# Moving one small transfer, the weights and the latents' blocks in the opening of a two-layer attention kernel

## The chip, the cores and the metric

The kernel is one program on one core of a Trainium2 chip. The metric is the device time of that program in microseconds; runs are compared by their medians. The engines named below are PE (matrix products, with its weight loads PEld), DVE, ACT and POOL (elementwise work, reductions and activation functions), and SP, whose queue issues most of the transfers.

## The reference

Two trunk layers work on 512 latent tokens and 256 context tokens of width 1024. Each layer normalises both streams, modulates them with a scale and a shift computed from a conditioning vector (one vector for the latents, one for the context), and projects them to 4608 columns. Three groups of heads attend on parts of that projection, a gate multiplies the result, and an output projection is added back. The part that matters here stands at the start of layer 0:

```
mod = c_silu @ ada_w + ada_b                     # shift, scale, gate, each 1024 wide
hx = rmsnorm(x, norm_w) * (1 + scale) + shift    # latents, 512 tokens
hc = rmsnorm(cx, norm_w) * (1 + scale_c) + shift_c   # context, 256 tokens
px = split_cols(hx @ w_in)
pc = split_cols(hc @ w_in)
rmsnorm(x, w) = x * rsqrt(mean(x*x) + 1e-6) * w
```

Group A also normalises its queries and keys per head with two rows of 64 weights per layer, and group C has one sink logit per head. These 272 numbers are the small input `bcast`.

## The kernel before

Activations lie with the 1024 features on partitions, as eight blocks of 128 features (index `kt`), and the tokens along the free axis: 512 columns of latents and 256 of context. All products are made in three passes of a rounded high part and a low part (`hh`, `hl` for activations, `wh`, `wl` for weights): high by high, high by low, low by high. `split` (line 244) makes the weight parts: a copy on ACT (line 247) and a subtraction (line 250, on DVE in the opening).

The opening of layer 0 (lines 381 to 461) runs like this.

- SP issues its transfers in the order of the program, one queue, with eight semaphores in turn, so that a ninth transfer waits for the first to land. In that order come `sm` (small constants), `bc` (the 272 numbers, spread over 128 partitions by an access pattern with a step of zero, line 81), the eight latent blocks `x` of 256 KB (`load_x(0)`), the first modulation weights `ada` (two halves of 512 KB), the eight context blocks of 128 KB (`load_x(1)`), and from there modulation weights of later blocks and projection weights `ws` of 256 KB.
- `norm_x` makes the sums of squares: for each block ACT squares it (line 351), and DVE adds the square onto the first one (line 355), so that seven additions follow each other. The squares have three buffers, of which one holds the sum. Then PE adds over partitions with a vector of ones (line 359), DVE and POOL make the inverse root (lines 366 and 369), PE spreads it over all partitions (line 378), and ACT copies it to `rb` (line 401).
- `ada(kt)` makes the modulation of one feature block: PE products in two halves (line 214), an ACT copy `adasb` (line 218), PE transposes (line 222), DVE sums and additions (lines 225 to 231).
- `make_h(kt, s)` makes the high and low part of one block of stream `s`: DVE scales `x` in place (line 408), ACT adds the shift and rounds to `hh` (line 409). For half of the blocks DVE makes `hl` (line 411), for the others POOL does it in two steps (lines 413 and 414): the latents of even `kt` go to DVE, those of odd `kt` to POOL. `wrap_h` repeats 64 columns of the latents.
- For each `kt`, PE then adds that block's products to eight open accumulators (line 430): `q` and `k` of head group B for latents (512 columns, in `pj`) and context (256, in `Obig`), and `v` per token tile (in `Sbig`). The contraction runs over `kt`, so no result is ready before the eighth block.
- `spread_silu` transposes the conditioning vector in four pieces (line 135), copies them on ACT (line 138) and stores them for later.

A tile scheduler places each engine's instructions by data, buffers and priorities, at build time. Each engine runs its list strictly in order. From the end of this opening on, PE has product after product, in both layers.

Of the kernel before, what the change touches and what calls it, by code (L numbers as in the profile page):

```python
# [15 lines left out]
OP = mybir.AluOpType  # L16
# [5 lines left out]
NT = 512  # L22
NCX = 256
# [34 lines left out]
BC_N = 272  # L58
# [5 lines left out]
def body(tc, xT, small, bcast, rpb, adaw, adat, wt, wf, wo, trigA, trigC, mskB, mskC, outT):  # L64
    nc = tc.nc
# [12 lines left out]
    sm = const.tile([128, SM_N], F32)  # L78
    nc.sync.dma_start(sm, small)
    bc = const.tile([128, BC_N], F32)  # L80
    nc.sync.dma_start(bc, bass.AP(tensor=bcast.tensor, offset=bcast.offset, ap=[[0, 128], [1, BC_N]]))
    ones = const.tile([128, 2], F32)
    nc.vector.memset(ones, 1.0)
    mhalf = const.tile([128, 8], F32)
# [1 line left out]
    onesw = const.tile([128, 64], F32)  # L86
    nc.vector.memset(onesw, 1.0)
    negsink = const.tile([128, 16], F32)
    nc.vector.tensor_scalar(negsink, bc[:, BC_SINK:BC_SINK + 16], -1.0, None, op0=OP.mult)

    def pj():
        return ps.tile([128, 512], F32, name="pj", bufs=CFG["pj"])
# [102 lines left out]
    def ada_load(k, pool, tag, bufs):  # L195
        sts = []
        for half in range(2):
            st = pool.tile([128, 4, 256], F32, name="ada", tag=tag, bufs=bufs)
            nc.sync.dma_start(st, adaw[k, half])
            sts.append(st)  # L200
        return sts
# [52 lines left out]
    def load_w1(dram_ap, i, shape):  # L254
        st = wpool.tile([128, 512], F32, name="ws", bufs=CFG["ws"])
        pace["sp"] = nc.sync.dma_start(st, dram_ap[:, i * 512:(i + 1) * 512]).ins.name
        return split(st, shape)
# [14 lines left out]
    def en(kind):  # L272

        turn[kind] = turn.get(kind, -1) + 1
        return nc.vector if EN[kind][turn[kind] % len(EN[kind])] == "D" else nc.gpsimd
# [14 lines left out]
    def wrap_h(kt):  # L290
        for h in (hh, hl):
            t = h[kt][2]
            nc.scalar.activation(t[:, 0:64], t[:, NT:NT + 64].bitcast(F32), AF.Copy)
# [7 lines left out]
    def off_tile(h, t):  # L301

        return h[2][:, t * 128:t * 128 + 128] if t < 4 else cols(h, t * 128, 128)
# [41 lines left out]
            with tc.high_priority(offset=CFG["hp"]):  # L345
                done(p[:, 0:512].rearrange("p (t c) -> p t c", t=2), t2)

    def add_sq(sums, x, kt, n, pool, bank=psO):

        sq = pool.tile([128, NT], F32, name="sq", bufs=3)  # L350
        nc.scalar.activation(sq[:, 0:n], x, AF.Square)
        if kt == 0:
            sums.append(sq)
            return
        en("sq").tensor_add(sums[0][:, 0:n], sums[0][:, 0:n], sq[:, 0:n])
        if kt == KT - 1:
            pss = bank()
            for t in range(n // 128):
                nc.tensor.matmul(pss[:, 2 * t:2 * t + 2], sums[0][:, t * 128:(t + 1) * 128], ones,
                                 start=(t == 0), stop=True, skip_group_check=True)  # L360
            sums.append(pss)
# [22 lines left out]
    with tc.tile_pool(name="p0", bufs=1, reuse_waits="tile") as p0:  # L384
# [3 lines left out]
        def load_x(s):  # L388
            c0, c1 = SETS[s]
            for kt in range(KT):  # L390
                x = p0.tile([128, c1 - c0], F32, name=f"x{s}", bufs=8)
                nc.sync.dma_start(x, xT[kt * 128:(kt + 1) * 128, c0:c1])
                xs[s, kt] = x

        def norm_x(s):
            n = SETS[s][1] - SETS[s][0]
            sums = []
            for kt in range(KT):
                add_sq(sums, xs[s, kt], kt, n, p0, lambda: Obig[:, s * 8:])
            r = p0.tile([128, n], F32, name=f"rb{s}")  # L400
            nc.scalar.activation(r, rstd_rows(sums[1], n, p0, Sbig[:, s * 512:s * 512 + n])[:, 0:n], AF.Copy)
            rb[s] = r
# [11 lines left out]
                nc.gpsimd.tensor_sub(hl[kt][s], x, hh[kt][s].bitcast(F32))  # L414


        load_x(0)
        sts = {0: ada_load(0, p0, "ada", CFG["a0"])}
        load_x(1)
        norm_x(0)  # L420
        norm_x(1)
        early["f", WF_BQ] = [pj(), Obig[:, 0:256]]
        early["f", WF_BK] = [pj(), Obig[:, 256:512]]
# [12 lines left out]
        for kt in range(KT):  # L436
            if kt < KT - 1:
                sts[kt + 1] = ada_load(kt + 1, p0, "ada", CFG["a0"])
            if kt % 4 == 0:
                wq = {s: load_w1(wf[0, s], kt // 4, (4, 128)) for s in (WF_BQ, WF_BK)}  # L440
            if kt % 2 == 0:
                wv = load_w1(wt[0, WT_BV, kt // 4], kt // 2 % 2, (2, 256))
            hh[kt], hl[kt] = new_h(), new_h()
            with tc.high_priority(offset=CFG["h1"]):
                ada(kt, sts.pop(kt), psT)
                for s in range(2):
                    make_h(kt, s)
                wrap_h(kt)
            for x, s in enumerate((WF_BQ, WF_BK)):
                wh, wl = wq[s]  # L450
                for g, (c0, n) in enumerate(((0, NT), (NT, NCX))):
                    for i, (a, b) in enumerate(((wh, hh), (wh, hl), (wl, hh))):
                        part(("c", 0) if g else ("l", x), early["f", s][g][:, 0:n], a[:, kt % 4, :], cols(b[kt], c0, n),
                             kt, i)
            wh, wl = wv
            for t in (1, 2, 3, 4, 5, 0):
                p = early["t", WT_BV][t // 2][:, t % 2 * 256:t % 2 * 256 + 256]
                for i, (a, b) in enumerate(((hh, wh), (hh, wl), (hl, wh))):
                    part(("v", t // 2), p, off_tile(a[kt], t), b[:, kt % 2, :], kt, i)
            if kt in (1, 2, 3, 4):  # L460
                spread_silu(kt - 1, p0)

# [1208 lines left out]
```

## Time and profile before

| | |
|---|---|
| median of 3 runs (lowest, highest) | 1202.65 us (1200.88, 1202.7) |
| span of the profiled execution | 1197.7 us |
| own time of the profiled execution | not given beside its span; the median of the runs lies 4.95 us above that span |
| PE, PEld busy | 1150.5 us (96%), 1034.8 us (86%) |
| DVE, ACT, POOL busy | 769.4 us (64%), 696.9 us (58%), 408.1 us (34%) |
| moved by transfers | 124.22 MB |

All times inside the program count from the start of the span. A row of the timeline gives start, duration, engine, line, operation, the tiles written and read, the shape and a count; rows of equal instructions that follow each other are merged, and the bracket at the end tells how long the engine had been idle and what ended that. A group row gives the busy time of a line's instructions and the mean nanoseconds of one. The chain of waits follows the work back from the last instruction, each step to what released it.

### The profile page before, as it was taken

How to read it: one execution, taken by the hardware profiler on the slowest of the kernel's cores; microseconds unless marked ns; L12 is line 12 of the kernel's file. 1: busy time of each engine (PE TensorE's matmuls, PEld its weight loads, DVE VectorE, ACT ScalarE, POOL GpSimd, SP SyncE). 2: the span in 40 equal slices, each digit the busy share in tenths (PEclk: the TensorE clock that was granted, in tenths of full speed). 3: DMA queues.
4: the chain of work that ended last, by engine and by line, in shares of the span. 5: the costliest groups of instructions: out<-in, count | busy, mean ns of one | idle time of the engine just before them, and what ended most of it. 6: DMA issues, size and time to landing. Idle time of an engine off the chain costs nothing.

```text
span 1197.7 us, 21749 instructions
## 1 busy us (share of the span) xinstructions
PE 1150.5 (96%) x8016; PEld 1034.8 (86%) x8016; DVE 769.4 (64%) x1548; ACT 696.9 (58%) x1581; POOL 408.1 (34%) x496
## 2 busy tenths in 40 slices
PE   5999999999999999999999999999999999998997
PEld 3898999998898988988778999989988888887876
DVE  5767566764656665568578895567754556567563
ACT  5446555656666676588423544555666667677552
POOL 1341110234446354385000030202274563656001
PEclk9999999999999999999999999999999999999999
DMA  9552222313312112123086662323222111232152
GB/s 321 213 142 89 78 78 67 123 66 104 111 70 92 67 44 92 34 63 119 27 293 198 205 210 74 98 84 109 91 73 67 53 46 53 63 88 72 36 161 77
DMA packets 60826, 124.22 MB, mean 104 GB/s; under 512 B 7216, under 2 KB 13488, under 8 KB 60720
## 3 DMA queue, kind: packets, MB, share of 16 engines
q1 hardware_dynamic: 54768, 111.96, 29.6%
q10 hardware_dynamic: 5952, 10.88, 2.7%
q8 instruction: 63, 1.03, 0.3%
q14 instruction: 43, 0.35, 0.1%
HBM read 109.05 MB, written 11.14 MB: 100 GB/s over the span
## 4 chain that ended last, share of the span: by engine, by line
PE 81%; DVE 5%; ACT 5%; DMA 3%; issue 3%; POOL 1%; SPq 0%; ACTq 0%; DVEq 0%; POOLq 0%
PE pj L318 18%; PE pj L341 17%; PE Sbig L1049 9%; PE Obig L1049 9%; PE T L1054 9%; PE pj L519 5%; PE T L519 3%; PE Sbig L519 3%; PE T L341 2%; PE Sbig L430 2%; DVE ptl L1044 1%; DMA x<-xT_dram 1%; PE Sbig L341 1%; ACT pth L798 1%; PE pj L430 1%
## 5 line engine op out<-in xcount | busy, mean ns | idle before, releaser
L1044 DVE TENSOR_TENSOR ptl<-T,pth 128x512 fp32r<-128x512 f32 (+2 forms) x312 | 181.1, 591 | 128.6 <-ACT pth L798 126.7
L798 ACT ACTIVATE pth<-T 128x512 fp32r<-128x512 f32 (+2 forms) x312 | 158.9, 520 | 134.8 <-PE T L1054 128.1
L341 PE MATMUL pj<-wh,hL 128*128 128x256 f32 x896 | 180.6, 287 | 0.0
L318 PE MATMUL pj<-hL,wh 128*128 128x512 f32 x544 | 175.0, 401 | 0.9 <-ACT wh L247 0.5
L1054 PE MATMUL T<-ident,P 128*128 128x128 f32 x1024 | 165.7, 273 | 4.0 <-ACT qt L902 1.7
L247 ACT ACTIVATE wh<-ws 128x512 fp32r<-128x512 f32 x192 | 119.5, 629 | 78.6 <-PE pj L318 16.3
L1049 PE MATMUL Sbig<-kt,qt 128*128 128x256 f32 (+1 forms) x864 | 156.2, 308 | 4.6 <-ACT P L1160 2.5
L250 POOL TENSOR_TENSOR wl<-ws,wh 128x512 fp32r<-128x512 f32 x76 | 98.5, 1300 | 146.4 <-ACT wh L247 146.4
L341 PEld LDWEIGHTS pj<-wh,hL 128*128 128x128 f32 x896 | 144.2, 190 | 1.0 <-issue 0.2
L1049 PE MATMUL Obig<-pth,vt 128*128 128x256 f32 (+2 forms) x432 | 134.6, 321 | 4.6 <-ACT pth L798 2.0
L1054 PEld LDWEIGHTS T<-ident,P 128*128 128x128 f32 x1024 | 123.0, 140 | 17.6 <-DVE ptl L1044 2.2
L1049 PE MATMUL Obig<-ptl,vt 128*128 128x256 f32 (+2 forms) x432 | 131.4, 318 | 5.0 <-DVE ptl L1044 4.3
L1049 PEld LDWEIGHTS Sbig<-kt,qt 128*128 128x128 f32 x864 | 123.3, 189 | 13.4 <-DVE negm L1208 4.1
L341 PE MATMUL pj<-wl,hL 128*128 128x256 f32 x448 | 128.0, 286 | 0.0
L318 PEld LDWEIGHTS pj<-hL,wh 128*128 128x128 f32 x544 | 96.2, 189 | 16.7 <-ACT wh L247 0.9
L250 DVE TENSOR_TENSOR wl<-ws,wh 128x512 fp32r<-128x512 f32 x116 | 82.7, 720 | 40.4 <-ACT wh L247 31.6
L318 PE MATMUL pj<-hL,wl 128*128 128x512 f32 x272 | 107.1, 394 | 0.5 <-DVE wl L250 0.5
L1049 PEld LDWEIGHTS Obig<-pth,vt 128*128 128x128 f32 x432 | 81.6, 189 | 15.9 <-ACT pth L798 7.1
L1049 PEld LDWEIGHTS Obig<-ptl,vt 128*128 128x128 f32 x432 | 81.5, 189 | 14.7 <-DVE ptl L1044 11.3
L1445 POOL TENSOR_TENSOR bm<-wr,bm 128x192 f32<-128x192 f32 (+1 forms) x48 | 41.3, 888 | 139.6 <-DMA bm<-mskB_dram 132.4
L341 PEld LDWEIGHTS pj<-wl,hL 128*128 128x128 f32 x448 | 85.4, 191 | 0.3
L1158 DVE TENSOR_REDUCE negm<-Sbig 128x1 f32<-128x768 f32 x64 | 61.0, 953 | 29.7 <-PE Sbig L1049 15.7
(336 smaller groups left out, 2495.6 us busy)
## 6 DMA issues: line engine op xcount, KB each, us to landing
ws<-wf_dram SPq DMA_DIRECT2D x72, 256.0 KB, 3.1
ws<-wt_dram SPq DMA_DIRECT2D x72, 256.0 KB, 3.0
ada<-adaw_dram SPq DMA_DIRECT2D x32, 512.0 KB, 5.5
ws<-wo_dram SPq DMA_DIRECT2D x57, 256.0 KB, 2.8
bm<-mskB_dram SPq DMA_DIRECT2D x16, 576.0 KB, 3.7
dw<-adat_dram SPq DMA_DIRECT2D x8, 512.0 KB, 8.2
dots<-adat_dram SPq DMA_DIRECT2D x16, 256.0 KB, 4.5
u<-u ACTq DMA_DIRECT2D x9, 384.0 KB, 2.9
```

The costliest lines, as they stand in the source:

```text
L247: nc.scalar.activation(hi, src, AF.Copy)
L250: eng.tensor_sub(lo, src, hi.bitcast(F32))
L318: paced(nc.tensor.matmul(p[:, 0:n], a[:, r, :], cols(b[kt], c0, n), start=(i == 0), stop=(i == 23)), i)
L341: paced(nc.tensor.matmul(p[:, t * 256:(t + 1) * 256], tok(a[kt], t2 + t), b[:, r, :], start=(i == 0), stop=(i == 23)), i)
L430: mm = nc.tensor.matmul(out, a, b, start=begin, stop=(kt == KT - 1 and i == 2), skip_group_check=True)
L519: mm = nc.tensor.matmul(p[:, 0:n], a[:, r, :], ucols(ua[b][ft], c0, n), start=(ft == FT_ORDER[0] and i == 0), stop=(ft == FT_ORDER[-1] and ...
L798: nc.scalar.activation(out, src, AF.Copy)
L1044: i = nc.vector.tensor_sub(lo[:, 0:n], T[:, 0:n], hi[:, 0:n].bitcast(F32))
L1049: m = nc.tensor.matmul(*args, **kw)
L1054: m = nc.tensor.transpose(*args, **kw)
L1158: nc.vector.tensor_reduce(nm, S, axis=AX.X, op=OP.max, negate=True)
L1445: nc.gpsimd.tensor_add(b, src, b)
```

## The change

- The row `bc` is no longer spread by the access pattern at the head of SP's queue. The host repeats the 272 numbers 128 times, and a plain transfer brings them in when the fifth feature block (`kt == 4`) is built; the small operation on it (`negsink`) goes with it.
- The seven additions of the latents' squares are cut by columns: DVE adds columns 0 to 383, POOL columns 384 to 511. The context's stay whole on DVE.
- `norm_x(0)` and the weights of the first block come before `load_x(1)` in the program, so the three `ws` transfers and their splitting stand ahead of the context's transfers and squares.
- `wrap_h` follows the latents directly, and for each `kt` all latent products (`q`, `k`, `v`) come before all context products.

```diff
-    nc.sync.dma_start(bc, bass.AP(tensor=bcast.tensor, offset=bcast.offset, ap=[[0, 128], [1, BC_N]]))
...
-    nc.vector.tensor_scalar(negsink, bc[:, BC_SINK:BC_SINK + 16], -1.0, None, op0=OP.mult)
...
-    def add_sq(sums, x, kt, n, pool, bank=psO):
+    def add_sq(sums, x, kt, n, pool, bank=psO, cut=0):
...
-        en("sq").tensor_add(sums[0][:, 0:n], sums[0][:, 0:n], sq[:, 0:n])
+        if cut:
+            nc.gpsimd.tensor_add(sums[0][:, cut:n], sums[0][:, cut:n], sq[:, cut:n])
+        nc.vector.tensor_add(sums[0][:, 0:cut or n], sums[0][:, 0:cut or n], sq[:, 0:cut or n])
...
-                add_sq(sums, xs[s, kt], kt, n, p0, lambda: Obig[:, s * 8:])
+                add_sq(sums, xs[s, kt], kt, n, p0, lambda: Obig[:, s * 8:], 0 if s else 384)
...
+        def load_weights(kt):
+            if kt % 4 == 0:
+                wq.update({s: load_w1(wf[0, s], kt // 4, (4, 128)) for s in (WF_BQ, WF_BK)})
+            if kt % 2 == 0:
+                wq["v"] = load_w1(wt[0, WT_BV, kt // 4], kt // 2 % 2, (2, 256))
+
+        wq = {}
         load_x(0)
         sts = {0: ada_load(0, p0, "ada", CFG["a0"])}
+        norm_x(0)
+        load_weights(0)
         load_x(1)
-        norm_x(0)
         norm_x(1)
...
+            if kt == 4:
+                nc.sync.dma_start(bc, bcast)
+                nc.vector.tensor_scalar(negsink, bc[:, BC_SINK:BC_SINK + 16], -1.0, None, op0=OP.mult)
...
                 for s in range(2):
                     make_h(kt, s)
-                wrap_h(kt)
-            for x, s in enumerate((WF_BQ, WF_BK)):
-                wh, wl = wq[s]
-                for g, (c0, n) in enumerate(((0, NT), (NT, NCX))):
+                    if s == 0:
+                        wrap_h(kt)
+            for g, (c0, n) in enumerate(((0, NT), (NT, NCX))):
+                for x, s in enumerate((WF_BQ, WF_BK)):
+                    wh, wl = wq[s]
...
-            for t in (1, 2, 3, 4, 5, 0):
-                p = early["t", WT_BV][t // 2][:, t % 2 * 256:t % 2 * 256 + 256]
+                wh, wl = wq["v"]
+                for t in ((4, 5) if g else (1, 2, 3, 0)):
+                    p = early["t", WT_BV][t // 2][:, t % 2 * 256:t % 2 * 256 + 256]
...
-    bcast = np.concatenate([q_norm_a.ravel(), k_norm_a.ravel(), sink_c.ravel()])
+    bcast = np.tile(np.concatenate([q_norm_a.ravel(), k_norm_a.ravel(), sink_c.ravel()]), (128, 1))
```

The scheduler turns this into other lists. At the head of SP's queue, before (128x512 are latent blocks, 128x256 context blocks):

```order
L79 DMA sm<-small_dram 128x88
L81 DMA bc<-bcast_dram 128x272
L392 DMA x_113<-xT_dram 128x512
...
L392 DMA x_127<-xT_dram 128x512
L199 DMA ada<-adaw_dram 128x1024 x2
L392 DMA x_133<-xT_dram 128x256
...
L392 DMA x_147<-xT_dram 128x256
L199 DMA ada<-adaw_dram 128x1024 x2
L256 DMA ws<-wf_dram 128x512 x2
L256 DMA ws<-wt_dram 128x512
```

And in the change:

```order
L79 DMA sm<-small_dram 128x88
L392 DMA x_111<-xT_dram 128x512
...
L392 DMA x_125<-xT_dram 128x512
L197 DMA ada<-adaw_dram 128x1024 x2
L254 DMA ws<-wf_dram 128x512 x2
L254 DMA ws<-wt_dram 128x512
L392 DMA x_192<-xT_dram 128x256
...
L392 DMA x_206<-xT_dram 128x256
L197 DMA ada<-adaw_dram 128x1024 x6
```

The row `bc` is gone from second place (it now stands as the 36th transfer), and the three `ws` went from behind the context's blocks and the second block's modulation weights to a place ahead of both.

On ACT, from the last square of a latent block to the first rounded block `hL`, before (`rb_176` is the latents' inverse root, `adasb` the copy for the modulation, `spr` a piece of `spread_silu`):

```order
L351 ACTIVATE sq<-x_127 128x512
L351 ACTIVATE sq<-x_133 128x256
...
L351 ACTIVATE sq<-x_139 128x256
L218 ACTIVATE adasb<-T 128x256
L351 ACTIVATE sq<-x_141 128x256
...
L351 ACTIVATE sq<-x_147 128x256
L401 ACTIVATE rb_176<-Sbig 128x512
L138 ACTIVATE spr<-T 128x512
L409 ACTIVATE hL<-x_113,mod_0_98 128x512
L247 ACTIVATE wh<-ws 128x512
```

In the change:

```order
L349 ACTIVATE sq<-x_125 128x512
L245 ACTIVATE wh<-ws 128x512 x2
L216 ACTIVATE adasb<-T 128x256
L245 ACTIVATE wh<-ws 128x512
L349 ACTIVATE sq<-x_192 128x256
L349 ACTIVATE sq<-x_194 128x256
L401 ACTIVATE rb_165<-Sbig 128x512
L349 ACTIVATE sq<-x_196 128x256
L349 ACTIVATE sq<-x_198 128x256
L136 ACTIVATE spr<-T 128x512
L349 ACTIVATE sq<-x_200 128x256
L409 ACTIVATE hL<-x_111,mod_0_96 128x512
```

The three weight copies moved ahead of `rb`; of the context's eight squares, two stand ahead of `rb`, three between `rb` and `hL`, and three behind.

On PE, from the start to the second feature block's modulation, before (`L214` are modulation products, `L359` the sums over partitions, `L430` the blocks' products):

```order
L214 MATMUL T<-ada,silu_c 2x256 x4
L359 MATMUL Obig<-ones,sq 128x2 x4
L214 MATMUL T<-ada,silu_c 2x256 x4
L222 MATMUL T<-ident,adasb 128x128 x2
L378 MATMUL Sbig<-ident,rstd 128x128 x4
L135 MATMUL T<-ident,silu_c 128x128 x4
L214 MATMUL T<-ada,silu_c 2x256 x4
L359 MATMUL Obig<-ones,sq 128x2 x2
L214 MATMUL T<-ada,silu_c 2x256 x4
L430 MATMUL pj<-hL,wh 128x512 x2
L222 MATMUL T<-ident,adasb 128x128 x2
```

In the change:

```order
L359 MATMUL Obig<-ones,sq 128x2 x4
L212 MATMUL T<-ada,silu_c 2x256 x8
L378 MATMUL Sbig<-ident,rstd 128x128 x4
L220 MATMUL T<-ident,adasb 128x128 x2
L133 MATMUL T<-ident,silu_c 128x128 x4
L438 MATMUL pj<-hL,wh 128x512 x2
...
L212 MATMUL T<-ada,silu_c 2x256 x4
L359 MATMUL Obig<-ones,sq 128x2 x2
L212 MATMUL T<-ada,silu_c 2x256 x8
L220 MATMUL T<-ident,adasb 128x128 x2
```

Before the first `pj` product the change has one block's modulation and the latents' sums; the second block's modulation (8), the context's sums (2) and the third block's modulation now stand between the first `pj` product and the second block's transposes (the last row), where before those transposes followed the first two products at once. Behind the opening the lists of all engines are the same but for a few neighbours that change places.

More of the change, by code (lines that the diff above doesn't have):

```diff
@@ L438, in body @@
                 sts[kt + 1] = ada_load(kt + 1, p0, "ada", CFG["a0"])
[L439 to L442, printed above, removed]
+            if kt:
+                load_weights(kt)
+            if kt == 4:
+                nc.sync.dma_start(bc, bcast)
+                nc.vector.tensor_scalar(negsink, bc[:, BC_SINK:BC_SINK + 16], -1.0, None, op0=OP.mult)
             hh[kt], hl[kt] = new_h(), new_h()
@@ L454, in body @@
                              kt, i)
-            wh, wl = wv
-            for t in (1, 2, 3, 4, 5, 0):
-                p = early["t", WT_BV][t // 2][:, t % 2 * 256:t % 2 * 256 + 256]
-                for i, (a, b) in enumerate(((hh, wh), (hh, wl), (hl, wh))):
-                    part(("v", t // 2), p, off_tile(a[kt], t), b[:, kt % 2, :], kt, i)
+                wh, wl = wq["v"]
+                for t in ((4, 5) if g else (1, 2, 3, 0)):
+                    p = early["t", WT_BV][t // 2][:, t % 2 * 256:t % 2 * 256 + 256]
+                    for i, (a, b) in enumerate(((hh, wh), (hh, wl), (hl, wh))):
+                        part(("v", t // 2), p, off_tile(a[kt], t), b[:, kt % 2, :], kt, i)
             if kt in (1, 2, 3, 4):
```

## The prediction

> **What bounds the kernel now.** I read the page first, for the engine that fills the span.
>
> ```profile
> PE 1150.5 (96%) x8016; PEld 1034.8 (86%) x8016; DVE 769.4 (64%) x1548; ACT 696.9 (58%) x1581; POOL 408.1 (34%) x496
> PE 81%; DVE 5%; ACT 5%; DMA 3%; issue 3%; POOL 1%; SPq 0%; ACTq 0%; DVEq 0%; POOLq 0%
> ```
>
> PE is busy 96% of the span and holds 81% of the chain that ends last. The change adds and removes no product, so it can gain only where PE waits. The chain in order of time shows where, in the opening:
>
> ```profile
> 2.58 5.51 DMA x<-xT_dram
> ...
> 8.11 6.29 DMA x<-xT_dram
> ...
> 15.36 6.04 DMA ws<-wf_dram
> ...
> 21.42 0.64 ACT wh L247
> ...
> 22.10 0.74 PE pj L430 x2
> ...
> 30.18 0.69 DVE mod L231
> ...
> 31.55 0.73 ACT hL L409
> 32.29 0.04 issue
> 32.33 0.74 PE pj L430 x2
> ...
> 33.89 0.83 PE Sbig L430 x7
> ```
>
> The first real product starts at 22.10, released by a weight copy that waited for its transfer. A second stall ends at 32.33. By stages:
>
> ```profile
> 22.10:32.33 10.23, 9.66 (x70) 5.70 (x71) 7.44 (x19) 5.38 (x14) 5.06 (x5) 1.00 1.03 407
> 32.33:69.08 36.75, 36.75 (x302) 32.28 (x303) 23.01 (x51) 18.09 (x45) 15.59 (x14) 1.00 0.54 181
> ```
>
> From 32.33 to the end of the opening PE is busy 36.75 of 36.75 us. So what the change is worth is how much earlier PE reaches the state that it has at 32.33: two latent products of the third block next, nothing missing any more.
>
> **The change, part by part.**
>
> *The row bc.* What the head of the queue costs stands in the transfers' list and in two stretches of 2.20 to 5.60 and 5.60 to 13.60 (last number: GB/s):
>
> ```profile
> bc<-bcast_dram SPq DMA_DIRECT2D x1, 136.0 KB, 4.8
> sm<-small_dram SPq DMA_DIRECT2D x1, 44.0 KB, 1.8
> 2.20:5.60 3.40, 0.00 (x0) 0.00 (x0) 0.65 (x6) 0.22 (x1) 0.00 (x0) 1.00 0.82 135
> 5.60:13.60 8.00, 0.73 (x8) 0.14 (x8) 5.02 (x8) 5.04 (x8) 0.00 (x0) 1.00 1.05 394
> 6.73 2.75 ACT L351 ACTIVATE sq<-x 128x512 f32<-128x512 f32 x4 [4.00 <-DMA x<-xT_dram]
> 8.12 5.47 DVE L355 TENSOR_TENSOR sq<-sq 128x512 f32<-128x512 f32 x7 [1.99 <-ACT sq L351]
> 9.65 0.63 ACT L351 ACTIVATE sq<-x 128x512 f32<-128x512 f32 x1 [0.17 <-DVE sq L355]
> ```
>
> While `bc` is under way the queue moves 135 GB/s, afterwards 394. ACT gets its first latent block at 6.73. Without `bc` ahead, the first block is issued when `bc` was, at about 1.17 (chain: 1.64 less one issue of 0.47), and lands after 1.8 (as `sm` did) and 256 KB at 394 GB/s (0.66): at 3.5 to 3.6. I take 3.5; bounds 3.2 to 4.2. That is 3.2 us earlier. The later load of `bc` I cost at nothing. 10.25 MB stand ahead of it in the queue, so at 394 GB/s it lands near 29.6; DVE comes to `negsink` behind the fourth block's scaling, near 32, and by its place in the order PE then has some 59 products of 0.12 (chain: 0.83 by seven) in hand. If that cover failed, DVE's next low part, queued behind `negsink`, would wait, and PE for it, at most for the 4.8 that `bc` takes now.
>
> *The additions cut by columns.* Now each takes 0.78 (5.47 by seven). For the new pair the trace has these rows:
>
> ```profile
> L355 DVE TENSOR_TENSOR sq<-sq 128x512 f32<-128x512 f32 x14 | 9.6, 689 | 4.1 <-ACT sq L351 3.4
> L355 DVE TENSOR_TENSOR sq<-sq 128x256 f32<-128x256 f32 x14 | 5.9, 421 | 2.5 <-ACT sq L351 2.3
> L1340 POOL TENSOR_TENSOR tR<-onesw,rec 128x128 f32<-128x128 f32 x30 | 11.1, 404 | 0.3 <-DVE rec L1327 0.3
> 550.99 1.28 POOL L492 TENSOR_TENSOR hL<-uf,hL 128x512 fp32r<-128x512 f32 x1 [0.90 <-ACT hL L491]
> 551.75 0.80 DVE L492 TENSOR_TENSOR hC<-uf,hC 128x256 fp32r<-128x256 f32 x1
> ```
>
> DVE alone would need 0.555 for 384 columns (middle of 0.689 and 0.421), POOL 0.40 for 128. But the last two rows show them in each other's way: POOL works until 552.27, and the DVE subtraction, which alone takes 0.42, starts inside that time and ends at 552.55, 0.28 after POOL. So DVE's reading waits for POOL's end, and only 0.14 of it lies beside. A pair then takes 0.40 + 0.555 − 0.14 = 0.82. The square after next needs the buffer that both release: 0.06 to start (the row at 9.65, behind the addition that ends at 8.12 + 0.78 + 0.69), 0.63 on ACT, 0.13 until DVE starts (8.12 after two squares from 6.73), and the pair's 0.82 make 1.64 for two pairs, 0.82 for each. I take that, so the cut gains nothing. The second block lands 0.66 after the first, at 4.17; the first addition starts at 4.17 + 0.63 + 0.13 = 4.93, and the last pair ends at 4.93 + 6 × 0.82 + 0.82 = 10.7, before 13.59: 2.9 us earlier. Bounds: without that wait 0.69 each, ending at 9.6; with the 0.1 that lies between two additions now (0.78 less 0.69) behind each pair, 0.92, ending at 11.3. Nothing else is queued on POOL then. The Trainium skill (SBUF — State Buffer, "Who interferes with whom") says that a DVE instruction with two SBUF inputs and a POOL instruction that reads SBUF exclude each other for the whole of the instruction; by that the pair would take 0.96, each step 0.89 by the same buffer sum, the last pair would end at 11.2, and the forecast would be 0.5 us higher. The row's 0.14 beside the other speaks for the smaller figure.
>
> *From the sums to the first product.* The rows:
>
> ```profile
> 12.87 1.03 PE L214 MATMUL T<-ada,silu_c 128*2 128x256 f32 x8 [12.87 <-DVE sq L355]
> 13.83 1.87 PE L359 MATMUL Obig<-ones,sq 128*128 128x2 f32 x8
> 15.98 1.03 POOL L369 TENSOR_TENSOR rstd<-rstd,mhalf 128x4 f32<-128x4 f32 x1 [14.70 <-DVE rstd L366]
> 18.89 0.58 ACT L401 ACTIVATE rb<-Sbig 128x512 f32<-128x512 f32 x1
> 20.41 0.72 ACT L409 ACTIVATE hL<-x,mod 128x512 fp32r<-128x512 f32 x1
> ```
>
> PE's sums (1.87) run to 12.5, and now both halves of the first modulation follow them (0.96 each from start to start of the next, 12.87 to 13.83) to 14.4; the root (1.03) is ready by 13.9, beside them. ACT, in order, waits for that modulation, copies it (0.4) to 14.9, then makes the third weight copy (0.6) and two context squares (0.4 each) before `rb` from 16.3 to 16.9. DVE, which has the modulation's sums and two context additions ahead, scales the block from 17.7 to 18.3; ACT meanwhile has two squares, `spr` and another square, and `hL` lasts from 18.6 to 19.35. First product at 19.4, 2.7 earlier than now. What releases PE today, the weights, has 3.25 MB up to its first block in the new queue: at 394 GB/s it lands near 11, and is copied before `rb`. That wait is gone, and `hL` is late next. The context's blocks land up to 2 us later for that (0.75 MB), from 13.3 on; ACT wants the first near 15.5.
>
> *From there to the steady state.* What PE waits for in this stretch is the second block's low part, made on POOL:
>
> ```profile
> 22.68 0.38 PE L222 MATMUL T<-ident,adasb 128*128 128x128 f32 x2
> 24.84 0.74 DVE L408 SCALAR_TENSOR_TENSOR x<-x,mod,rb 128x512 f32<-128x512 f32 x1
> 25.62 0.72 ACT L409 ACTIVATE hL<-x,mod 128x512 fp32r<-128x512 f32 x1 [0.51 <-DVE x L408]
> 26.45 2.48 POOL L413 TENSOR_SCALAR x<-x,mod 128x512 f32<-128x512 f32 x2 [3.68 <-ACT hL L409]
> 28.89 1.27 POOL L414 TENSOR_TENSOR hL<-x,hL 128x512 fp32r<-128x512 f32 x1
> ```
>
> It is ready at 30.16. In the change more stands on PE between the first product and the transposes (L222): two products and a half modulation to 20.3, when the first block's low part is there; four products (0.9), the other half (0.5), the context's sums (0.5), the third block's modulation (1.0). So the transposes start near 23.3 instead of 22.68. From there to DVE's scaling it takes 2.2 today (22.68 to 24.84), with two weight subtractions between, each as long as an addition of 512 columns (0.7), which in the change are done by then; 2.2 less 1.4, and 0.2 for waits, is 1.0: 24.3. ACT has three copies ahead of `hL` (25.2 to 25.9); POOL takes the same 3.7: ready at 29.8, only 0.4 earlier. Four products (0.9 with their start) follow to 30.9. In the old order the same products are followed by a wait until 32.33 for the third block. Here the third block's modulation is made with the second's, so its high part is ready near 28.2 and its low part near 30.6, and PE goes on. 32.33 − 30.9 = 1.4 us.
>
> The other half, context products behind latent ones, moves no count: the same 30 products for each block. Behind the opening the lists are the same, so 1.4 reaches the end: span 1197.7 − 1.4 = 1196.3, and with the 4.95 that the runs' median lies above this span, 1201.3. Own range: gain 0.5 to 2.3, 1200.4 to 1202.2.
>
> A measurement of this kernel tells about 0.2%, 2.4 us, from no change.
>
> **The rivals.**
>
> 1. The start is carried in full: POOL's low part isn't what PE waits for (its transposes come earlier than I placed them), and PE is dense from 19.4. Then the gain is 2.7 at the first product, and up to 3.5 with the 0.57 that PE isn't busy between 22.10 and 32.33: 1199.2 to 1200.0. For it: the transfers of the second and third block's modulation come 2 to 5 us earlier, since weights and `bc` are out of their way. Against: the order of PE. Chance 0.26.
> 2. DVE and POOL add side by side: 1.0 more, gain 2.4, 1200.3, half of it over the bound. Against: the pair at 551. Chance 0.12.
> 3. The clock, slower than before. These rows are at the layer's end and in the opening (the number before the last two is the granted clock):
>
> ```profile
> 621.76:625.17 3.41, 0.79 (x3) 0.35 (x3) 3.37 (x7) 1.46 (x3) 0.00 (x0) 1.00 1.02 375
> 625.20:628.50 3.30, 3.30 (x8) 2.63 (x9) 3.30 (x6) 1.26 (x2) 0.00 (x0) 0.50 1.01 367
> 18.57 1.06 PE L135 MATMUL T<-ident,silu_c 128*128 128x128 f32 x4
> 23.88 0.60 PE L135 MATMUL T<-ident,silu_c 128*128 128x128 f32 x4
> ```
>
> After 3.4 us with PE busy 0.79, the granted clock was 0.50 for 3.3 us. The same four transposes took 1.06 at 18.57 and 0.60 at 23.88: PE sped up between, just before its first product. In the change PE has nothing to do from about 17.5 to 19.4 and less fill work before. If it then runs at half speed for one stretch of 3.4 us, 1.7 less 0.5 of slack are lost, gain 0.2 (1202.4); for two, 3.4 less 0.5, a loss of 1.5 (1204.1); from 8.7 us at half speed it passes the bound. The Trainium skill (TensorE: Matmul & The Clock Gate, part 1) says that the clock is raised after one busy window of about 3.4 us and lowered after an idle one, with windows that run freely; by that rule one window is the usual price. The trace's 3.3 us at 0.50 agree. Chance 0.12, of which 0.05 over the bound.
> 4. The change doesn't do what it says: the first transfers crawl whatever they are, and the blocks come only 0.35 earlier (136 KB at 394 GB/s). Then nothing is left, 1202.6. Against: `sm` landed in 1.8. Chance 0.06.
>
> **How the numbers follow.** The forecast has 0.44: 1201.3. Faster by over 0.2% (under 1200.25): 0.26 of rival 1, 0.06 of rival 2, 0.02 of the forecast's edge, 0.34. Slower by over 0.2%: 0.05. The rest, 0.61, is the same. Range: down to rival 1 with its first block at the early bound (1199.0), up past one slow stretch of the clock, half-way to two (1203.3).
>
> **What would show it.** Right: first `x` lands near 3.5; the pairs of additions every 0.8, DVE's or POOL's stretched over 0.55 or 0.40; first product near 19.4; a wait of PE for POOL's `hL` (L414) near 29 to 30; dense from there. Wrong: additions ending before 10 (rival 2), no such wait and a dense PE from 20 (rival 1), products of 512 columns that take twice as long after 19 (rival 3), a first block after 5 (rival 4), or a difference behind 70 us that the opening does not have.

## The result and the profile after

| | before | changed |
|---|---|---|
| median of 6 runs each, side by side | 1200.81 us | 1205.12 us |
| ratio of the runs, 95% interval | | 1.0038 (1.0024 to 1.0051) |
| span of the profiled execution | 1197.7 us | 1203.7 us |

The change makes the kernel slower by 0.38%, some 4.5 us (4.3 between the medians); the forecast was 1.4 us faster. Two single runs on record, one of the kernel before (1894.1 us) and one of an experiment below (row and cut additions, 2284.5 us), lie far off all others and enter no ratio. The first lines of the changed kernel's page: PE does the same 8016 products, and DMA and POOL have taken some of its share of the chain.

```profile
PE 1153.2 (96%) x8016; PEld 1036.6 (86%) x8016; DVE 770.8 (64%) x1548; ACT 697.2 (58%) x1581; POOL 415.4 (35%) x503
PE 79%; DVE 6%; ACT 5%; DMA 4%; issue 3%; POOL 3%; SPq 0%; ACTq 0%; DVEq 0%; POOLq 0%
```

I read the end of the opening at the first product of the projection behind it. The row of the chain before, and that of the changed kernel:

```profile
86.12 5.47 PE pj L318 x24
```
```profile
90.61 5.47 PE pj L316 x24
```

It comes 4.49 later: in these two executions the opening loses as much as the medians do. (The two spans differ by 6.0: this execution was at half clock for 6.8 us near 629 and for 3.4 us near 1014, the one before for 3.4 us near 625; such stretches come and go between executions.) The chain of the changed kernel in order of time:

```profile
2.58 5.67 DMA x<-xT_dram
...
12.77 1.86 PE Obig L359 x8
14.64 1.81 PE T L212 x16
...
20.00 0.71 ACT hL L409
...
20.75 1.04 PE pj L438 x2
...
22.76 1.90 PE pj L438 x4
...
26.72 0.39 PE T L220 x2
...
28.83 0.62 ACT hL L409
...
29.55 3.07 POOL x L413 x2
32.62 1.24 POOL hL L414
...
33.90 2.58 PE pj L438 x10
```

The first product is 1.35 earlier than before (20.75 against 22.10), but the second block's transposes (L220) come at 26.7 against 22.7, and a wait for POOL's low part ends at 33.9 (the forecast had its end at 29.8; before, that part was ready at 30.2 and PE, busy until then, did not wait for it). The chain goes on with a second wait of that kind, that the forecast did not have at all:

```profile
54.80 0.55 PE T L212 x8
55.35 0.38 PE T L220 x2
...
57.39 0.73 ACT hL L409
...
58.21 2.07 POOL x L413
60.28 0.04 issue
60.32 0.92 POOL x L413
61.24 1.50 POOL hL L414
62.74 0.04 issue
62.79 1.19 PE pj L438 x4
```

How much PE stood idle from its first instruction to the end of the opening shows in the stretches (elapsed, then PE's busy time), before and changed:

```profile
12.87:85.96 73.09, 71.72 (x567) 59.80 (x568) 49.45 (x112) 37.50 (x89) 29.87 (x30) 1.00 0.64 220
```
```profile
12.77:90.44 77.67, 72.42 (x566) 59.56 (x567) 48.98 (x112) 37.65 (x89) 33.26 (x31) 0.98 0.59 203
12.77:17.58 4.81, 4.79 (x29) 3.29 (x30) 1.66 (x4) 2.32 (x5) 1.76 (x2) 1.00 0.94 292
20.99:24.40 3.41, 3.41 (x14) 1.35 (x13) 1.77 (x4) 1.14 (x5) 0.00 (x0) 0.50 1.03 416
```

Idle time rose from 1.37 to 5.25 us. That is 3.88 of the 4.58 by which this stretch is longer. The two largest parts of it, in the list of what PE waited for (us in total, times, longest), are the two waits for POOL's low part and one wait ahead of the first product; the kernel before had 0.6 of the second kind and none of the first:

```profile
PE pj L438 <- POOL hL L414: 1.9, 2, 1.0
PE pj L438 <- ACT hL L409: 1.7, 1, 1.7
```

The half clock took about as much in both: the records of the clock begin with its first change (the column reads 1.00 ahead of that), but the durations show it: L212 x16 lasts 1.81 at 14.64, and 0.97 at 25.74. I count half of the time that PE is busy at half clock as lost: 4.79 and 3.41 make 4.10 here, and 7.54 up to 21.01 make 3.77 before. This count is an estimate of PE's own time, not of the kernel's: where PE would have waited anyway, its slowness costs nothing.

### The profile page after: what moved, and what is told of

Read it like the earlier page. It is cut to its first block, busy times and chain, and to the rows that moved or that the text cites. A ratio compares the mean times of both kernels' runs of the same rounds, so it can differ in the third digit from the quotient of the medians.

```text
span 1203.7 us, 21771 instructions
## 1 busy us (share of the span) xinstructions
PE 1153.2 (96%) x8016; PEld 1036.6 (86%) x8016; DVE 770.8 (64%) x1548; ACT 697.2 (58%) x1581; POOL 415.4 (35%) x503
## 4 chain that ended last, share of the span: by engine, by line
PE 79%; DVE 6%; ACT 5%; DMA 4%; issue 3%; POOL 3%; SPq 0%; ACTq 0%; DVEq 0%; POOLq 0%
PE pj L316 17%; PE pj L339 17%; PE Sbig L1059 9%; PE Obig L1059 9%; PE T L1064 9%; PE pj L529 5%; PE T L529 3%; PE Sbig L529 3%; PE T L339 1%; PE Sbig L438 1%; DMA dots<-adat_dram 1%; PE pj L438 1%; DVE ptl L1054 1%; PE Sbig L339 1%; ACT pth L808 1%
```

## The experiments

Every kernel ran beside the kernel before on the same chip. "Idle" and "half clock" are counted as above, in each kernel's one profiled execution, from PE's first product that isn't a filler to the end of the opening; the ratio, over all runs, is what decides. (Fillers are products of a constant ahead of all other work on PE; the early and the late place are two places in PE's order. Both are explained below.) The profiled execution is one of the runs, and not always a typical one: with the late place mended it took 1210.8 us, the slowest of 12 with a median of 1206.3, with both mended 1204.2 against 1201.2.

| kernel | ratio to before (95%) | first block product | idle | half clock | end of opening |
|---|---|---|---|---|---|
| before | 1 | 22.10 | 1.4 | 3.8 | 85.96 |
| changed | 1.0038 (1.0024, 1.0051) | 20.75 | 5.2 | 4.1 | 90.44 |
| row alone | 0.9993 (0.9977, 1.0008) | 21.42 | 0.9 | 5.9 | 85.75 |
| row and cut additions | 1.0002 (0.9990, 1.0014) | 21.05 | 1.2 | 6.3 | 86.00 |
| weights first alone | 1.0061 (1.0044, 1.0078) | 21.51 | 5.2 | 4.6 | 90.51 |
| order of products alone | 1.0020 (1.0010, 1.0031) | 22.05 | 0.6 | 6.6 | 86.97 |
| changed, not weights first | 1.0000 (0.9983, 1.0016) | 22.87 | 1.2 | 6.5 | 87.77 |
| changed, old order of products | 1.0067 (1.0045, 1.0088) | 19.44 | 5.8 | 4.3 | 89.87 |
| changed, whole additions | 1.0043 (1.0031, 1.0055) | 20.63 | 4.5 | 5.8 | 89.92 |
| changed, late place mended | 1.0039 (1.0022, 1.0057) | 20.56 | 3.9 | 9.5 | 93.13 |
| changed, early place mended | 1.0029 (1.0016, 1.0042) | 20.61 | 4.2 | 5.8 | 90.33 |
| changed, both mended | 1.0009 (0.9997, 1.0020) | 20.70 | 3.1 | 8.0 | 90.85 |
| before, 34 fillers | 1.0000 (0.9992, 1.0009) | 21.61 | 1.2 | 4.6 | 86.17 |
| changed, 34 fillers | 1.0026 (1.0010, 1.0042) | 19.21 | 5.6 | 3.9 | 89.67 |
| row alone, 34 fillers | 0.9994 (0.9984, 1.0004) | 20.02 | 3.6 | 1.6 | 84.96 |
| row alone, 44 fillers | 0.9985 (0.9972, 0.9997) | 21.26 | 2.0 | 1.7 | 85.06 |
| both mended, 44 fillers | 1.0008 (0.9995, 1.0021) | 19.37 | 4.9 | 2.7 | 88.97 |

### Which part of the change loses

My theory from the two traces was W, that the place of the first weights does it; the rivals were the order of the products and the cut additions. Taking `load_weights(0)` and `norm_x(0)` back behind `load_x(1)`, all else as changed:

```diff
-        norm_x(0)
-        load_weights(0)
         load_x(1)
+        norm_x(0)
         norm_x(1)
...
-            if kt:
-                load_weights(kt)
+            load_weights(kt)
```

> The changed kernel with load_x(1) ahead of norm_x(0) and the first weights behind both, as before; row, cut additions and the order of products as changed. Theory W: what was lost comes back, the opening ends at 84 to 86.3 us, time 0 to 2 us under the kernel before. Rival O: it ends at 88 to 91. Rival S (POOL's share of the additions costs it, by the lock with DVE): first block product later than 22.1 and the end at 87 or later.

Measured: 1.0000 (0.9983 to 1.0016). The loss is gone, and the two waits for POOL's low part with it; what PE waits for in this kernel, up to 90 us (us in total, times, longest; the first line is the start):

```profile
PE Obig L359 <- DVE sq L355: 13.3, 1, 13.3
PE Obig L437 <- ACT hC L409: 0.6, 1, 0.6
PE T L133 <- DVE mod L223: 0.6, 1, 0.6
```

The end of the opening was 87.77, past theory W's 86.3, and the first block product came at 22.87: the two marks of rival S, that POOL's share of the additions costs it. The half clock may explain them (6.5 us against 3.8 in the trace before); the time speaks against S, and so do the two runs on the additions below. The same part the other way round, alone in the kernel before (the row still at the head, whole additions, old order of products):

> The kernel before with only the first weights (and norm_x of the latents) put ahead of the context's transfers; the row at the head, whole additions, old order of products. Theory W: this part alone loses: PE idle in the opening over 4 us, the fourth conditioning piece and the last blocks' modulation late in its list, the end of the opening at 89 to 92, time 3 to 7 us over the kernel before. Rival: it takes the earlier start too (the weights wait on nothing while the latents are late): within 1 us of the kernel before.

Measured: 1.0061, a little more than expected, idle 5.2 us, and the two waits for POOL are there:

```profile
PE pj L438 <- POOL hL L414: 2.0, 2, 1.1
```

So this part alone is enough for the loss, and without it there is none that can be told. The part holds two moves, `load_weights(0)` and `norm_x(0)`, both put ahead of `load_x(1)`; neither was tried by itself. The row alone, with its `negsink`, and the order of products taken back out of the changed kernel:

> The kernel before with the row bc alone moved and replicated (no cut additions, weights and products in the old order). I read the end of the opening at the first product of the first projection behind it (line 318 of the kernel before), which starts at 86.12 us in the trace before and at 90.61 in the changed one. Theory W (the weights' place costs it): the row alone does no harm, the first product of the blocks comes at 20.8 to 22.1 and the end of the opening at 84.5 to 86.3, time 0 to 1.6 us under the kernel before. Rival P (the row's new place disturbs the later loads): end at 88 or later.

> The changed kernel with the old order of products (weight by weight, context beside latents) and wrap_h behind both; everything else of the change kept, the weights ahead of the context too. Theory W: the order of the products is not the cause, the opening ends at 89 to 92 us, time 3 to 6 us over the kernel before. Rival O (latents ahead of context cost it, since context products no longer stand between to cover the waits): it ends at 85 to 87, time within 1 us of the kernel before or below.

Measured: 0.9993 for the row alone, no difference that can be told; and 1.0067 with the old order of products (8 us, more than the 3 to 6 expected), so the new order is not the cause of the loss. That it eases it is not shown, since the two intervals overlap. The additions, whole in the changed kernel, and cut beside the row alone:

> The changed kernel with the latents' additions whole on DVE again. Theory: the cut is worth nothing on the chip (e8 against e1 by 0.06%, inside the intervals), additions every 0.78, time 3 to 6 us over the kernel before, like the changed kernel. Rival: POOL's share holds back the start, or the order made with it is the harmful one: within 1.5 us of the kernel before.

> The row late and the additions cut by columns, weights and products in the old order. My forecast had the cut at nothing (a pair every 0.82 us, against 0.78 before). In the changed kernel's trace the pairs come every 0.73 to 0.84 and POOL's part takes 0.66 to 0.82 beside DVE. Theory: the same time as the row alone, within 1 us; additions every 0.75 to 0.85. Rival S (POOL and DVE add side by side once ACT is not held up by transfers): additions every 0.65, the sums on PE 0.7 to 1 us earlier than with the row alone.

Measured: 1.0043 and 1.0002. The cut neither helps nor harms by more than the intervals of some 0.12%. Beside the row alone the pairs came every 0.79 us, not 0.65 as under rival S. The last addition did end 0.8 earlier than with the row alone (11.68 against 12.47), as S had it, but in that execution the eighth block had landed 0.9 earlier (9.58 against 10.45). The order of products alone in the kernel before:

> The kernel before with only the new order of products (latents ahead of context, wrap_h behind the latents). Theory W: no loss of its own, since the kernel with the old order of products and all the rest lost more (0.67%) than the changed one: within 1.2 us of the kernel before, end of the opening less half clock at 81.5 to 83.5. Rival: latent products bunched ahead leave nothing to cover the waits for POOL's low parts: 2 us or more over.

Measured: 1.0020, 2.4 to 2.8 us over, where theory W had expected at most 1.2; the rival's mark of 2 us was met. But the rival's mechanism, waits for POOL's low parts, isn't in the trace: PE is idle for 0.6 us, less than before, and waits for POOL nowhere. What it pays with I can't tell; with the row, the cut and this order together the time is 1.0000.

### Why weights first lose: queue or order

The weights change two things: the order of the transfers in SP's queue, and the order that the scheduler makes of PE's instructions. There, the third block's modulation got ahead of the second block's transposes (shown with the change), and the last three blocks' modulation bunched up. These are rows of the changed kernel's list on PE, with products between them left out:

```
61 L220 MATMUL T<-ident,adasb 128x128 x2
...
118 L133 MATMUL T<-ident,silu_c 128x128 x4
119 L212 MATMUL T<-ada,silu_c 2x256 x8
...
134 L212 MATMUL T<-ada,silu_c 2x256 x4
135 L220 MATMUL T<-ident,adasb 128x128 x2
136 L212 MATMUL T<-ada,silu_c 2x256 x4
137 L220 MATMUL T<-ident,adasb 128x128 x2
138 L212 MATMUL T<-ada,silu_c 2x256 x8
```

Between the fifth block's transposes (row 61) and the sixth's (135) stand 56 rows of the blocks' products, at 118 the fourth conditioning piece, and only from 119 on the modulation. In the kernel before the transposes of the fifth to the eighth block are spread: rows 84, 119, 137 and 160. I mended the two places, the late one, the early one, and both, and left the loads where they were. (In the traces the first 46 loads on SP's queue keep their order; with the late place mended, the fourth conditioning piece is stored three places earlier, and a few loads from there on change places.)

```diff
             if kt in (1, 2, 3, 4):
-                spread_silu(kt - 1, p0)
+                with tc.high_priority(offset=CFG["h1"]):
+                    spread_silu(kt - 1, p0)
```
```diff
+                    if k == 2:
+                        after(mm, turned[1])
...
+            turned[k] = tr.ins.name
```

In the second one `turned[1]` names the last of the second block's transposes.

> The changed kernel with spread_silu called at the priority of the modulation, so that the fourth transposition of the conditioning vector no longer stands behind 76 rows of products and in front of the last three blocks' modulation. If the late wait (PE idle between 55 and 63 us, released by POOL's low part) comes from that piece, it goes, the modulation of the last blocks stands between 38 and 55 us, and the opening ends at 87.5 to 89 us, 1.6 to 3.1 earlier than in the changed kernel. If that wait has another cause (the transfers, POOL), it stays and the opening ends at 90 to 91.

> The changed kernel with only the first of the two mends: the third block's modulation tied behind the second block's transposes; the fourth conditioning piece and the last blocks' modulation as late as in the changed kernel. Theory R1 (the early place carries the loss): the late waits near 56 and 62 us stay (1.5 us), but the wait near 33 goes, and the time lies 0.5 to 2.5 us over the kernel before. Rival R2 (the late place carries it, and the early one only with it): 3.5 to 6 us over, as the changed kernel.

> The changed kernel, every transfer and every part of the change where it is, but its order on PE mended at two places: the third block's modulation is tied behind the second block's transposes, and spread_silu has the priority of the modulation, so that the last blocks' modulation is spread over the stretch from 35 to 60 us again. Theory R (the weights cost through the order that the scheduler makes of them, not through the queue): PE idle in the opening falls from 5.2 to 1.5 to 3.5 us, the late waits near 56 to 62 go, and end of the opening less what the half clock takes (86.3 in the changed kernel) falls to 83 to 84.5; time 0 to 2.5 us over the kernel before. Rival Q (the transfers' order does it: the second block's modulation weights land 2 us later): the second block's transposes stay at 25.5 or later whatever the order, less half clock 85.5 or more, time 4 us or more over.

Measured: the late place alone 1.0039, the early place alone 1.0029 (3.5 us by the ratio, 4.3 by the medians: R2's mark, though R2's late place alone brought nothing), both 1.0009. In the traces each mend takes its own wait away: with the early place mended the wait near 33 is gone and the late one is left, with the late place mended it is the other way round. PE's busy time from 50 to 66 us, in the changed kernel and with both mended:

```profile
50.00:66.00 16.00, 14.49 (x125) 10.72 (x124) 9.63 (x25) 6.06 (x15) 7.67 (x6) 1.00 0.20 67
```
```profile
50.00:66.00 16.00, 16.00 (x127) 12.94 (x126) 10.67 (x26) 7.06 (x17) 7.31 (x6) 1.00 0.14 50
```

With the late place alone the expected end (87.5 to 89) was missed: 93.13. That execution was at half clock until 30.0 and again from 36.8 to 40.2, right behind a wait of 1.5 us for POOL:

```profile
36.81:40.23 3.42, 3.42 (x9) 2.64 (x10) 3.31 (x9) 2.23 (x6) 3.12 (x4) 0.50 0.97 388
```

Less the half clock its end is 93.13 − 9.54 = 83.6, against 90.44 − 4.10 = 86.3 in the changed kernel, 2.7 less; but such a difference is no measure of what the mend would bring at full clock (see the fillers below), and over 12 runs it brought nothing. Only both mends together bring most of the loss back, with the loads where the change puts them: PE is idle for 3.1 us (1.5 to 3.5 expected), and the end less the half clock is 82.9 (83 to 84.5 expected). So the time speaks for theory R, that the loss comes by the order. Rival Q's first mark did show, the second block's transposes at 26.66 with both mended, though PE had work without a gap from 20.70 to there, all of it at half clock; the time, 4 us or more over by Q, is against it. What was not tried is the two mends in a kernel without the weights ahead: if they made that one faster too, some loss by the transfers could be hidden behind them. How the loss divides between the places I leave open: 0.0009 and nothing alone, 0.0029 together, each interval about ±0.0015.

### What the half clock takes

Since all traces worked at half clock far into the opening, I put products of a constant ahead of everything on PE, into accumulator space that nothing reads, ahead of the scheduler, so that no other instruction moves.

```diff
+    one = nc.const_aps.tensor(1.0, [128, 1], F32)
+    with nc.psum_tensor([128, 512], F32) as warm:
+        for _ in range(34):
+            nc.tensor.matmul(warm[:, 0:128], one.to_broadcast([128, 128]), one.to_broadcast([128, 128]), start=True, stop=True)
     with tile.TileContext(nc, schedule_with_timeline_sim=bool(CFG["tl"])) as tc:
```

> The kernel before with 34 products of a constant (128x128, fp32, into accumulator space that nothing reads) ahead of everything on PE, no other instruction moved. In the traces so far PE works at a granted clock of 0.50 up to 21.0 us (before), 24.2 (row alone) and 26.8 (no weights first), which costs 3.8 to 6.5 us of the opening (half of the time that PE is busy at half clock). Theory G (the clock is raised only after PE has been busy for a stretch, so the opening is slow because PE has nothing to do ahead of 12.9): the sums on PE take 0.9 to 1.0 instead of 1.87, the first projection behind the opening starts at 82 to 84.5 instead of 85.96 (86.12 in the chain), time 2 to 5 us under the kernel before. Rival: the opening's end is set by transfers and POOL's low parts, PE's speed is slack: within 1 us.

> The changed kernel with the same 34 products ahead, nothing moved. If the changed kernel loses mainly by the half clock (a stretch of 3.4 us at 21.0), it comes within 1 us of the kernel before with the same products. If it loses by the waits that its order brings (theory W: PE idle 5.2 us in the opening against 1.4), it stays 3 to 5 us over that one, while 1 to 4 us under the changed kernel without them.

> The row bc alone moved and replicated, and the 34 products ahead. In the trace of the row alone the first product of PE came 1.0 us earlier, idle time fell from 1.4 to 0.9, and 2.1 us more were lost to the half clock (5.85 against 3.78). Theory G: with the clock up, the row's gain shows: 0.5 to 2 us under the kernel before with the 34 products, 3 to 6 under the kernel before. Rival: the row is worth nothing even so: the same as the kernel before with the products, within 0.5.

Measured: 1.0000, 1.0026 and 0.9994. Theory G's gain didn't come. The changed kernel stays over the kernel before with the same fillers, by 2.9 us between the means of 12 runs and 1.4 between the medians, less than the 3 to 5 expected; in the two traces the half clock takes about as much (3.9 and 4.6) and the idle time is 5.6 against 1.2, so the waits are what sets these two traces apart. The row's 0.06% is inside the interval. The kernel before with the fillers, its stretches and three rows of PE:

```profile
3.89:10.08 6.19, 6.19 (x55) 6.00 (x54) 2.26 (x5) 3.22 (x6) 0.00 (x0) 1.00 1.00 364
10.72:14.13 3.41, 1.54 (x16) 1.06 (x16) 2.12 (x4) 1.26 (x2) 0.00 (x0) 1.00 1.05 375
14.13:24.37 10.24, 9.23 (x48) 5.21 (x48) 6.88 (x22) 7.62 (x18) 1.97 (x2) 0.50 0.98 343
```
```profile
0.76 9.32 PE L1669 MATMUL warm<-const-float32-1.0 128*128 128x128 f32 x68 [0.76 <-PEq L1662]
...
13.21 1.05 PE L359 MATMUL Obig<-ones,sq 128*128 128x2 f32 x8
14.19 1.03 PE L214 MATMUL T<-ada,silu_c 128*2 128x256 f32 x8
```

The fillers raised the clock at 3.9, and the sums took 1.05 instead of 1.87. But they ended at 10.08, PE was busy for 1.54 of the next 3.41, and from 14.13 the clock was at half again, for three stretches. With 44 fillers, on the row alone and on both mends:

> The row alone moved and replicated, with 44 products of a constant ahead. With 34 of them it ran 0.06% under the kernel before (interval -0.16% to 0.04%), and its trace lost 3.9 us to the half clock, of which 1.6 lie behind the fillers. Theory G: the clock stays up between fillers and sums, end of the opening at 82.5 to 84.5, time 1.5 to 4 us under the kernel before. Rival: the gaps of 1 to 1.6 us behind the sums lower it all the same: 84.5 to 86, time within 1 us of the kernel before.

> The same with 44 products of a constant ahead on PE, which last to 11.6 to 13.1 us (34 of them ended at 10.08, ten more at 0.23), so that no idle stretch of 2.4 us lies between them and the sums, as lowered the clock again at 14.1 with 34. Theory G: granted clock 1.00 through most of the opening, 2 to 4 us less lost to the half clock, 1 to 3 us under the same kernel without them. Rival: waits on ACT, DVE and POOL take up what PE gains: within 1 us of it.

Measured: 0.9985 and 1.0008. In the first the half clock behind the fillers is down to one stretch (16.37 to 19.78, 1.7 us lost), and this kernel is 0.15% (1.8 us) under the kernel before, inside theory G's 1.5 to 4; its end, 85.06, is not (82.5 to 84.5) and lies in the rival's 84.5 to 86. Against the row alone without fillers (0.9993) it can't be told apart. On the mended kernel the fillers bring nothing, as the rival said: the time is the same, with 2.7 us at half clock instead of 8.0 and 4.9 idle instead of 3.1. (The clock was lowered at 18.0, behind a step with waits of 1.0 for the modulation and 0.8 for `hL`.)

So taking the half clock away does not shorten the opening by what the count says. For the row alone the 34 fillers took it from 5.9 to 1.6 us, but idle time rose from 0.9 to 3.6 and the end came only 0.8 earlier: most of what PE saved came back as waiting.

## Why the prediction was wrong, point by point

- **The first blocks** (3.5, then 0.66 apart): the first landed at 4.27, just past my bound of 4.2, but the fourth only at 8.26, not 5.5. The stretch from the first transfers to there moved 301 GB/s, not 394:

```profile
2.20:8.26 6.06, 0.00 (x0) 0.00 (x0) 1.77 (x8) 2.10 (x4) 1.57 (x2) 1.00 0.99 301
```

  In the 13 traces without the row at the head the first block landed at 3.60 to 4.27 and the fourth at 6.40 to 8.74; in the four with it, at 6.33 to 6.71 and 8.35 to 8.76. Some of rival 4 was true: the first block came 2.4 earlier than before, but the fourth only 0.5 and the eighth 0.55 (10.89 against 11.44). Of the 2.9 us that I had at the end of the last addition 0.6 was left in this execution (13.03 against 13.60), 1.1 in that of the row alone (12.47). The first weights, that I had near 11, landed at 14.1; ACT still waited for the modulation behind them, so this cost nothing.
- **The cut** at nothing: right. Where the transfers allowed it, with row and cut alone, pairs came every 0.73 to 0.84 (forecast 0.82, before 0.78). But it is POOL that waits, not DVE:

```profile
L355 DVE TENSOR_TENSOR sq<-sq 128x384 f32<-128x384 f32 x7 | 4.0, 567 | 5.6 <-ACT sq L349 5.5
L354 POOL TENSOR_TENSOR sq<-sq 128x128 f32<-128x128 f32 x7 | 5.2, 736 | 6.6 <-ACT sq L349 6.3
```

  DVE's part took its own 0.57, POOL's 0.74 instead of 0.40. Six of the seven pairs lasted 0.87, one of them from 9.03 (DVE) to 9.90 (POOL); that is between my 0.82 and the 0.96 that the rule of the Trainium skill (SBUF — State Buffer, "Who interferes with whom") gave.
- **The first product** at 19.4: 20.75 here, from the late blocks. The path from the end of the sums on had the right steps but took 6.1 (14.64 to 20.75), not 6.9 (12.5 to 19.4). With the old order of products, where the fourth block landed at 6.95, the product came at 19.44; that this is the forecast's number is luck, since the sums there ended 0.8 late and the path was 0.8 short.
- **The second block's transposes** at 23.3: the first step behind the start that failed. They came at 26.7. Of the 3.4 us, 1.35 are the late start, and 2.0 the stretch between (5.9 instead of 3.9): PE had no gap there, but ran it at half clock from 20.99 to 24.40, 1.7 of them. That is rival 3's mechanism, at a chance of 0.12: PE idle from 17.9 to 20.75 but for 0.62, and the clock halved for one stretch. I had put the third block's modulation into the sum, but only at full clock.
- **POOL's low part** at 29.8: 33.86. The same 3.4, and 0.6 more since its two steps at L413 took 3.07 instead of 2.48. In the kernel before this was no wait of PE's, as I had read it: PE had other products until 30.57, when the part was ready, and its one wait there, 0.57 until 32.33, was for the third block's high part (ACT).
- **"PE goes on"**, dense to the end of the opening: this is the step that failed for good, and the experiments name its cause, the order that came with the weights. I had read the new order on PE only up to the second block and took the rest of the opening for the old one. The bunched modulation of the last blocks brought 1.5 us of waits (0.55 near 56 and 0.95 ahead of 62.79). With the 4.1 at POOL's low part that makes 5.6 of the 5.9 us between forecast (1.4 earlier) and trace (4.49 later).
- **The base**: "4.95 above the span" was no constant. In the runs that list both, 1.7 to 2.1 us lie around the span (1205.51 with a span of 1203.7); by that the profiled execution before took some 1199.6, an estimate, and was one of the faster ones. The forecast's size did not hang on it.
- **The later load of the row** at nothing: right. It landed at 35.28, and `negsink` stood at 37.27 without a wait.
- **Behind the opening** nothing: nothing there asks for another cause. The 1.5 us between the two traces stand beside stretches of half clock that differ from execution to execution.

No chance of mine stood for what decided: an order in which PE waits twice for POOL, at 33.9 and at 62.8. Rivals 1 and 2 priced a better start; the slower side had only the clock, at 0.05. The idle stretch ahead of the first product I had seen (17.5 to 19.4), but priced only through the clock.

## What to carry to other kernels

One moved group of loads gave this scheduler's list another order on PE far behind it, up to the eighth block; the order has to be read to the end of the stage, looking for the distance between each block's preparation and its use, and not only around the moved lines. A gain at the start of a chain that is fed by blocks is worth nothing if the preparation of the later blocks slips behind the work that should cover it. And time that a slow clock takes from an engine that also waits can't be added up: here most of what the fillers saved came back as idle time.

## What the runs showed of the hardware that I had not expected

**What counts as work for the clock.** The granted clock changed only in steps of 3.41 us whose phase differed from execution to execution, as the Trainium skill (TensorE: Matmul & The Clock Gate, part 1) has it. It says that one busy window raises the clock. In the trace with both places mended, three consecutive windows of PE, the clock being raised at 30.36:

```profile
20.12:23.53 3.41, 2.83 (x12) 1.23 (x13) 2.32 (x6) 1.96 (x6) 0.00 (x0) 1.00 1.01 401
23.53:26.94 3.41, 3.41 (x18) 1.80 (x16) 0.10 (x1) 0.38 (x1) 0.00 (x0) 1.00 1.02 402
26.94:30.36 3.42, 3.42 (x24) 1.69 (x23) 1.34 (x6) 1.08 (x3) 0.70 (x1) 1.00 1.00 361
```

The second was busy for all of its 3.41 us and did not raise it (the modulation products behind it, from 27.26, took 1.89; the same 16 took 1.04 at full clock in the changed kernel). What sets it apart is the sums' products of two columns that stand in it (L364 here):

```profile
23.53:26.94 3.41, 1.01 (x4) 0.93 (x4) 1.00 1.02 402
26.94:30.36 3.42, 0.00 (x0) 0.00 (x0) 1.00 1.00 361
```

Counting PE's busy time from start to start and leaving out these two-column products, the first 40 us of all 17 traces agree: windows at half clock with at least 2.88 us of work raised it, those with up to 2.86 did not; at full clock windows with up to 1.69 us lowered it, those with at least 2.10 kept it. No run varied this alone, so the part of the two-column products is argued from the windows, not shown by an experiment. By it the context's sums in the opening keep the clock at half for one window more unless they fall across a border, and the profiled execution before was lucky there: 3.8 us at the count above, where the traces of the row alone, of the row and cut, and of the changed kernel without weights first come to 5.9 to 6.5.

**The scatter between executions goes with the clock.** Of 32 runs of the kernel before in one session those with a mean clock of 0.998 took 1199.2 us on the average, with 0.996 1200.5, with 0.994 1201.8, and the one with 0.991 1207.5; the correlation is −0.74 (−0.48 over the 19 of another session).
